# Activation copies put off, two early query blocks, and 1/rms taken with tokens on partitions, in a one-core decoder layer

## The chip, the cores and the metric

One core of one Trainium2 chip runs the whole program. The metric is the device time of one execution in microseconds (us); of several runs the median counts. The engines are named as in the profile: PE (TensorE, its weight loads shown apart as PEld), DVE (VectorE), ACT (ScalarE), POOL (GpSimd) and SP, whose queue issues most DMA transfers.

## The reference, cut to what matters

512 tokens, model width 1024, one layer:

```
h    = rmsnorm(x, norm1_g) * (1 + scale1) + shift1
p    = h @ w_in                          # q, k, v and the three conv inputs
attn = sliding-window attention(q, k, v) # 512 wide
conv = cb * short_conv(cc * cu)          # 512 wide
x    = x + gate1 * ([rmsnorm(attn) | rmsnorm(conv)] @ w_out)
h2   = rmsnorm(x, norm2_g) * (1 + scale2) + shift2
q    = h2 @ peer_wq                      # 8 heads x 2 halves x 128
sc   = q . subkeys                       # 128 scores per half, then top 16, pairs, top 16 again
x    = x + gate2 * sum over the chosen experts of softmax * gelu(u . h2) * v
```

with `rmsnorm(x, g) = x / sqrt(mean(x * x) + eps) * g`, the mean over the width of one token. Four such norms matter here: the first (over x), the conv norm, the attention norm (each 512 wide), and the second (over the updated x).

## The kernel before, in words

Activations lie transposed: the 128 partitions hold a block of the width, and the 512 tokens run along the free axis, so that `xT` is 8 tiles of 128x512. Products with a weight matrix are made exact enough by three passes: each factor is split into a rounded part and a rest (`split`, lines 175 to 177: ACT writes the rounded part, DVE the rest), and `mm3` (lines 197 to 202) issues three matmuls of 512 columns for each block of the depth. A block of 128 output columns therefore takes 24 matmuls. Weights come by SP's queue into five buffers and are split into four pairs of buffers.

A norm needs the sum of squares over the width, that is over partitions and blocks. Before, ACT squares the blocks, and a matmul with a 128x128 matrix of ones (lines 237, 253, 551 and 552) sums them over the partitions and at once repeats the sum on every partition, a 128x512 result in PSUM. `rstd` (lines 239 to 243) takes the square root of it on ACT and the reciprocal on DVE, both over 128x512, though all partitions hold the same 512 numbers.

The stages around the change, in order of the text:

- The first norm (from line 249), then the modulated activations `hH`, `hL`. The ones matmul stands on PE ahead of the matmuls that make the first modulation rows (`psr`, line 272).
- The input projection, attention and convolution follow the written list `PLAN` (line 50). `S` squares the conv output, `N` makes its norm (`part_norm`, line 463), `B2` and `B3` are the last two attention blocks (transposes, line 416, and products, line 425).
- The attention norm, squares and ones matmuls, at lines 518 to 520. Then `out_half(b, 0)`, the conv half of the output product, for four column blocks (48 matmuls), and `part_norm` of the attention half. The other half and the other blocks follow, each with its update of `xT` (line 544) and a running sum of squares.
- The second norm (lines 549 to 552 and 575). `spill` (line 528) transposes the updated x back, 32 transposes, and stores it. They wait for the last ones matmul (`end`).
- Then for each of 8 depth blocks `modulated` (line 226) makes `f` on DVE (x times scale times 1/rms), `fH` on ACT and `fL` on DVE. With `EARLY = 1`, one query block's three matmuls for that depth block follow at once on PE (line 582). Then `f` is transposed for two token groups (`pg`, line 593, 16 transposes), copied out, and 16 copies on ACT (line 598) put the first 352 tokens of `fH` and `fL` into `h2H` and `h2L`, which only `first()` (line 609, the u-side product of the experts) reads.
- The query loop (line 749), 16 turns: `query(hp)` makes the query block (24 matmuls), copies it out (`qs`, ACT), and `scores(hp - 1)` multiplies the block before with its subkeys (`psc`, line 739), copies the scores (ACT), and takes the top 16 of three token groups on DVE (`level1`, `level2`).
- After that the expert stages: `first`, `build`, `gated`, `second`, with gathered rows fetched by POOL.

The tile framework sets the waits and the order. A planner lays out each engine's instructions when the kernel is built, by its own model of durations. It goes by the order of the text where several instructions are ready, and takes a later one ahead where an earlier one still waits in its model. On the chip each engine then runs its list in that fixed order. PSUM has eight banks here: six of the pool `psm` (`bank`), two of `psa`.

Of the kernel before, what the change touches and what calls it, by code (L numbers as in the profile page):

```python
# [7 lines left out]
F32 = mybir.dt.float32  # L8
# [5 lines left out]
AF = mybir.ActivationFunctionType  # L14
# [4 lines left out]
P = 128  # L19
# [16 lines left out]
RING = 3  # L36
LOOK = 3
SPILL = 68
EARLY = 1
STB = 2  # L40
LD = 5
AHEAD = 7
# [47 lines left out]
def body(tc, p):  # L90
# [19 lines left out]
    def bank(name):  # L110
        return psm.tile([P, 512], F32, tag="m", name=name)
# [104 lines left out]
    def tmp(name):  # L216
        return tp.tile([P, T], F32, name=name, **T2)

    def squared(b, so_far=None):
        q = tmp("sq")  # L220
        nc.scalar.activation(q, b, AF.Square)
        if so_far is not None:
            nc.vector.tensor_add(q, q, so_far)
        return q
# [9 lines left out]
    def square(ps, b, i, n, w=None):  # L234
        q = tmp("sq")
        nc.scalar.activation(q, b, AF.Square)
        nc.tensor.matmul(ps, ones if w is None else w, q, start=(i == 0), stop=(i == n - 1))

    def rstd(ps, n):
        r = tmp("rstd")  # L240
        nc.scalar.activation(r, ps, AF.Sqrt, scale=1.0 / n, bias=eps)
        nc.vector.reciprocal(r, r)
        return r
# [2 lines left out]
    adabv = S("ada_b").rearrange("p (a k) -> p a k", a=6)  # L246


    ps = bank("ss1")
    sq = None  # L250
    for k in range(DC):
        sq = squared(xT[:, k, :], sq)
    nc.tensor.matmul(ps, ones, sq, start=True, stop=True)
    r1 = rstd(ps, D)
    hH = a1.tile([P, DC, T], F32R, tag="hH", name="hH")
    hL = a1.tile([P, DC, T], F32R, tag="hL", name="hL")
    hh, hlo = (lambda k: hH[:, k, :]), (lambda k: hL[:, k, :])
# [202 lines left out]
    vT = tmp("vT")  # L460
    nc.scalar.activation(vT, pj[5], AF.Copy)
    kg = S("kg")
    def part_norm(ss, src, g, o):
        r = rstd(ss, 512)
        for k in range(4):
            f = tmp("f")
            nc.vector.scalar_tensor_tensor(f, src[:, k, :], S(g, k), r, op0=OP.mult, op1=OP.mult)
            split(mH[:, o + k, :], mL[:, o + k, :], f)
# [12 lines left out]
    for step in PLAN.split():  # L481
        n = [int(x) for x in step[1:]]
        match step[0]:
            case "k":
                nk = qk1(pj[4], qk0(pj[4]), kg)
            case "q":
                nq[n[0]] = q0(pj[n[0]], n[0])
            case "P":
                pj[n[0]] = proj(n[0])
            case "V":  # L490
                pt = bank("vt")
                for c in range(NCH):
                    nc.tensor.transpose(pt[:, c * P:(c + 1) * P], vT[:, c * P:(c + 1) * P], ident)
                nc.scalar.activation(vN.rearrange("p a b -> p (a b)"), pt, AF.Copy)
            case "r":
                qk2(nq.pop(n[0]), qT[:, n[0], :])
            case "R":
                qk2(nk, kT)
            case "T":
                nc.scalar.activation(rq, ssq, AF.Sqrt, bias=eps64)  # L500
                nc.vector.reciprocal(rq, rq)
            case "A":
                sa[n[0]] = attend1(n[0])
            case "B":
                attend2(n[0], sa[n[0]])
            case "C":
                conv(*n)
            case "M":
                more_ada()
            case "S":  # L510
                ssc = bank("ssc")
                for k in range(4):
                    square(ssc, convT[:, k, :], k, 4)
            case "N":
                mH = a1.tile([P, DC, T], F32R, tag="hH", name="mH")
                mL = a1.tile([P, DC, T], F32R, tag="hL", name="mL")
                part_norm(ssc, convT, "cg", 0)
    ssa = bank("ssa")
    for k in range(4):
        square(ssa, attnT[:, k, :], k, 4)  # L520
    for b in range(HEAD):
        out_half(b, 0)
    part_norm(ssa, attnT, "ag", 4)
# [11 lines left out]
            nc.scalar.activation(xn, ps, AF.Copy)  # L535
            nc.sync.dma_start(x1s[c][:, half * 512:(half + 1) * 512], xn)

    ss2 = bank("ss2")
    sq = None
    for b in range(DC):  # L540
        if b >= HEAD:
# [6 lines left out]
        if b < 6:  # L548
            more_ada(3)
    sq = squared(xT[:, 6, :], sq)  # L550
    nc.tensor.matmul(ss2, ones, sq, start=True, stop=False)
    end = nc.tensor.matmul(ss2, ones, squared(xT[:, 7, :]), start=False, stop=True)
    nc.vector.tensor_add(mod[:, 24:48], mod[:, 24:48], ab[:, 24:48])
    nc.vector.scalar_tensor_tensor(s2, mod[:, 32:40], 1.0, S("n2g"), op0=OP.add, op1=OP.mult)
    a1_s.close()
# [16 lines left out]
    hx, hx_s = pool("hx")  # L572
    fH = hx.tile([P, DC, T], F32R, name="fH")
    fL = hx.tile([P, DC, T], F32R, name="fL")
    r2 = rstd(ss2, D)
    spill(0, end)
    spill(1, end)
    early = [(weights_of(p["wq"][b]), bank("pq")) for b in range(EARLY)]
# [5 lines left out]
    for r, (dst, cs) in enumerate(((hN, slice(TD - P, TD)), (h2N, slice(TD, T)))):  # L584
# [8 lines left out]
            nc.tensor.transpose(pg[k // 4][:, (k % 4) * P:(k % 4 + 1) * P], f[:, cs], ident)  # L593
        for k in range(2):
            nc.scalar.activation(dst[:, k * 512:(k + 1) * 512], pg[k], AF.Copy)
    for k in range(DC):
        for d, x in ((h2H, fH), (h2L, fL)):
            nc.scalar.activation(d[:, k, :], x[:, k, 0:TU].bitcast(F32), AF.Copy)

    xp_s.close()  # L600
    tp_s.close()
    r4, r4_s = pool("r4", side="right")
# [119 lines left out]
    def query(hp):  # L722
        sk = rp.tile([P, P], F32, tag="sk", name="sk", bufs=3)
        if hp < EARLY:
            ps = early[hp][1]
        else:
            w = weights_of(p["wq"][hp])
            ps = bank("pq")
            mm3(ps, w, lambda k: fH[:, k, :], lambda k: fL[:, k, :])
        nc.sync.dma_start(sk, p["sk"][hp])  # L730
        qs = tmp("qs")
        nc.scalar.activation(qs, ps, AF.Copy)
        return qs, sk
# [13 lines left out]

    last = None
    for hp in range(16):
        now = query(hp)  # L750
        if last:
            scores(hp - 1, *last)
        last = now
    scores(15, *last)
    weights(ND, Rd)
# [365 lines left out]
```

## Time and profile before

| | before |
|---|---|
| median of 3 runs | 1454.32 us (1452.81 to 1461.66) |
| profiled execution | 1453.08 us, of which span 1451.3 us |
| busy PE, PEld, DVE, ACT, POOL | 1394.5, 1224.8, 1240.8, 616.3, 405.3 us |
| from the start to the second norm's last ones matmul | 233.7 us |
| first subkey matmul of the query loop | at 258.8 us |

The span is the time between the first and the last recorded instruction of one profiled execution; 1.8 us of that execution lie around it. Busy time of PE is modelled at the ends of matmuls, which are pipelined: a busy PE can still have small stalls inside. A duration is that of one instruction, while the distance between the starts of two in a row is shorter where they overlap. A wait that the profile names is idle time of an engine, put down to what came last.

### The profile page before, as it was taken

The page shows a single profiled execution, that of the slowest core. Times are in us where ns is not written, and L with a number is a line of the kernel's source. Part 1 is how long each engine was busy: PE and PEld are TensorE (multiplying, and loading weights), DVE is VectorE, ACT ScalarE, POOL GpSimd, SP SyncE. Part 2 cuts the span into 40 slices and gives each one's busy share as a digit, 9 for nine tenths or more (in the row PEclk, how much of TensorE's full clock was granted, in tenths as well). Part 3 has the DMA queues.
Part 4 walks back from the last instruction along what each step waited for, and adds up shares of the span by engine and source line. Part 5 has one row for each costly group of instructions (what it writes and reads, how often), then busy time and mean ns, then how long its engine had stood idle before and what let it go on. Part 6 is the DMA issues. An engine that isn't in the chain of part 4 may idle for free.

```text
span 1451.3 us, 21225 instructions
## 1 busy us (share of the span) xinstructions
PE 1394.5 (96%) x7696; PEld 1224.8 (84%) x7696; DVE 1240.8 (85%) x2267; ACT 616.3 (42%) x1041; POOL 405.3 (28%) x292
## 2 busy tenths in 40 slices
PE   6999998999898999798999999999999999999998
PEld 4676776788898999798988888889899999999997
DVE  7778977899999999898568888988889898889944
ACT  4524636433634556364433333433343334333431
POOL 0000000000022320511024454446646455555300
PEclk9999999999999999999999999999999999999999
DMA  7645544222586997899989999999999999999843
GB/s 276 225 158 181 194 140 170 85 96 77 176 306 239 372 381 260 309 345 343 326 301 381 401 402 373 405 344 371 341 400 360 387 352 381 386 337 402 295 130 131
DMA packets 134376, 418.80 MB, mean 289 GB/s; under 512 B 12800, under 2 KB 39552, under 8 KB 132736
## 3 DMA queue, kind: packets, MB, share of 16 engines
q1 hardware_dynamic: 92800, 266.45, 51.1%
q0 software_dynamic: 41472, 151.01, 27.5%
q8 instruction: 60, 0.98, 0.3%
q14 instruction: 44, 0.36, 0.1%
HBM read 375.77 MB, written 41.62 MB: 288 GB/s over the span
## 4 chain that ended last, share of the span: by engine, by line
PE 22%; issue 14%; POOL 8%; DMA 7%; DVE 5%; ACT 0%; POOLq 0%; DVEq 0%; ACTq 0%
POOL row L773 8%; DMA row<-in_uR,eG 5%; PE pa L200 4%; PE pa L202 4%; PE pa L201 4%; PE o L990 3%; PE o L991 3%; PE o L989 3%; DMA row<-in_vL,eG 2%; DVE lo L177 2%; DVE junk L781 1%; DVE wwl L177 0%; DVE ga L905 0%; DMA raw<-in_vL 0%; DVE x L1008 0%
## 5 line engine op out<-in xcount | busy, mean ns | idle before, releaser
L176 ACT ACTIVATE hi<-raw 128x1024 fp32r<-128x1024 f32 x298 | 312.2, 1053 | 303.2 <-PE pa L201 83.9
L177 DVE TENSOR_TENSOR lo<-raw,hi 128x1024 fp32r<-128x1024 f32 x298 | 362.4, 1217 | 49.2 <-ACT hi L176 48.7
L200 PE MATMUL pa<-h2H,hi 128*128 128x352 f32 x1024 | 336.1, 328 | 21.1 <-ACT sp L621 21.1
L202 PE MATMUL pa<-h2H,lo 128*128 128x352 f32 x1024 | 332.8, 325 | 0.4 <-DVE lo L177 0.4
L201 PE MATMUL pa<-h2L,hi 128*128 128x352 f32 x1024 | 332.0, 324 | 0.0
L989 PE MATMUL o<-hi,wwh 128*128 128x512 f32 x768 | 299.5, 390 | 0.0
L990 PE MATMUL o<-lo,wwh 128*128 128x512 f32 x768 | 299.1, 389 | 0.2 <-DVE lo L177 0.2
L991 PE MATMUL o<-hi,wwl 128*128 128x512 f32 x768 | 298.9, 389 | 0.3 <-DVE wwl L177 0.3
L773 POOL DMA_INDIRECT row<-in_uR,eG x128 | 188.9, 1476 | 326.1 <-PE o L991 165.7
L781 DVE SCALAR_TENSOR_TENSOR junk<-row,h2N 128x1024 bf16<-128x1024 f32 x128 | 153.9, 1220 | 72.9 <-DMA row<-in_uR,eG 72.7
L200 PEld LDWEIGHTS pa<-h2H,hi 128*128 128x128 f32 x1024 | 194.8, 190 | 25.1 <-ACT sp L621 22.8
L773 POOL DMA_INDIRECT row<-in_vL,eG x128 | 171.7, 1341 | 145.6 <-PE o L991 91.3
L201 PEld LDWEIGHTS pa<-h2L,hi 128*128 128x128 f32 x1024 | 195.3, 191 | 2.2
L202 PEld LDWEIGHTS pa<-h2H,lo 128*128 128x128 f32 x1024 | 195.2, 191 | 0.7 <-DVE lo L177 0.7
L905 DVE SCALAR_TENSOR_TENSOR ga<-row,av,ga 128x1024 f32<-128x1024 f32 x127 | 163.0, 1283 | 25.6 <-DMA row<-in_vL,eG 24.5
L773 POOL DMA_INDIRECT row<-in_uR,eH x32 | 44.5, 1392 | 489.3 <-ACT sp L621 394.8
L991 PEld LDWEIGHTS o<-hi,wwl 128*128 128x128 f32 x768 | 144.1, 188 | 30.9 <-DVE wwl L177 0.7
L990 PEld LDWEIGHTS o<-lo,wwh 128*128 128x128 f32 x768 | 144.2, 188 | 28.7 <-DVE lo L177 0.6
L989 PEld LDWEIGHTS o<-hi,wwh 128*128 128x128 f32 x768 | 144.2, 188 | 28.2 <-issue 0.2
L176 ACT ACTIVATE wwh<-w 128x768 fp32r<-128x768 f32 x64 | 54.1, 845 | 156.9 <-DVE w L972 123.3
L971 ACT ACTIVATE w<-G 128x32 f32<-128x32 f32 x128 | 22.3, 222 | 196.3 <-DVE wwl L177 191.6
L177 DVE TENSOR_TENSOR wwl<-w,wwh 128x768 fp32r<-128x768 f32 x64 | 60.8, 951 | 10.5 <-ACT wwh L176 10.5
(265 smaller groups left out, 1831.2 us busy)
## 6 DMA issues: line engine op xcount, KB each, us to landing
raw<-in_uL SPq DMA_DIRECT2D x128, 512.0 KB, 6.2
raw<-in_vL SPq DMA_DIRECT2D x128, 512.0 KB, 6.9
Gd<-st SPq DMA_DIRECT2D x12, 2048.0 KB, 10.4
G<-Gd SPq DMA_DIRECT2D x16, 1536.0 KB, 11.7
ada<-in_ada SPq DMA_DIRECT2D x32, 512.0 KB, 4.2
Ad<-sp SPq DMA_DIRECT2D x34, 352.0 KB, 6.5
sp<-Ad SPq DMA_DIRECT2D x34, 352.0 KB, 7.1
raw<-in_w_in SPq DMA_DIRECT2D x18, 512.0 KB, 4.9
```

Source lines behind the costliest of these rows:

```text
L176: nc.scalar.activation(h, f, AF.Copy)
L177: nc.vector.tensor_sub(l, f, h.bitcast(F32))
L200: nc.tensor.matmul(ps, wh(k), rh(k), start=(k == k0), stop=False)
L201: nc.tensor.matmul(ps, wh(k), rl(k), start=False, stop=False)
L202: mark[0] = nc.tensor.matmul(ps, wl(k), rh(k), start=False, stop=(k == k1))
L773: d = nc.gpsimd.indirect_dma_start(out=t, out_offset=None, in_=tab, in_offset=bass.IndirectOffsetOnAxis(ap=e, axis=0))
L781: return nc.vector.scalar_tensor_tensor(junk, t, 1.0, h, op0=OP.mult, op1=OP.mult, accum_out=a)
L905: nc.vector.scalar_tensor_tensor(ga, t, av[:, k:k + 1], ga, op0=OP.mult, op1=OP.add)
L971: nc.scalar.activation(wv[:, i, nu:], g[:, i, nu:], AF.Copy)
L989: nc.tensor.matmul(o, wh[:, cs], vh[:, hs], start=(j == 0), stop=False)
L990: nc.tensor.matmul(o, wh[:, cs], vl[:, hs], start=False, stop=False)
L991: last = nc.tensor.matmul(o, wl[:, cs], vh[:, hs], start=False, stop=(j == NJ - 1))
```

## The change

Three edits. `EARLY` goes from 1 to 2, so that two query blocks accumulate while the second norm's activations are made. The 16 copies into `h2H` and `h2L` leave their place behind the transposes and go into the query loop, two behind the scores of each turn from the third to the tenth, each with a wait for the last product matmul that stood in the text ahead of that turn's query block. And the four norms over the width (first, conv, attention, second) use `token_rstd`: the squares are the stationary factor and one column of ones the moving one, chunk of 128 tokens by chunk, so that the sums come out with tokens on partitions, 128x4. The square root and the reciprocal work on 128x4. A product with the identity spreads these numbers on diagonals (`dg`, 128x512), and one matmul with ones repeats them on all partitions in a PSUM bank, which the users then read. The attention norm's squares stay where they were, but its matmuls now stand in `part_norm`, behind the 48 matmuls of the four half products; those of the conv norm stand in `N`, behind `B2`. The q and k norms are as before.

```diff
--- before.py
+++ after.py
@@ -36,7 +36,7 @@
 RING = 3
 LOOK = 3
 SPILL = 68
-EARLY = 1
+EARLY = 2
 STB = 2
 LD = 5
 AHEAD = 7
@@ -236,6 +236,27 @@
         nc.scalar.activation(q, b, AF.Square)
         nc.tensor.matmul(ps, ones if w is None else w, q, start=(i == 0), stop=(i == n - 1))
 
+    def token_rstd(qs, n, pl):
+
+
+        ps = bank("ss")
+        for c in range(NCH):
+            for i, q in enumerate(qs):
+                end = nc.tensor.matmul(ps[:, c:c + 1], q[:, c * P:(c + 1) * P], ones[:, 0:1], start=(i == 0),
+                                       stop=(i == len(qs) - 1))
+        r = cp.tile([P, 16], F32, tag="r", name="r", bufs=2)[:, 0:NCH]
+        nc.scalar.activation(r, ps[:, 0:NCH], AF.Sqrt, scale=1.0 / n, bias=eps)
+        nc.vector.reciprocal(r, r)
+        dg = tmp("dg").rearrange("p (c n) -> p c n", c=NCH)
+        sd = [P, NCH, P]
+        nc.vector.tensor_mul(dg, ident[:, None, :].to_broadcast(sd), r[:, :, None].to_broadcast(sd))
+        out = pl()
+        nc.tensor.matmul(out, ones, dg, start=True, stop=True)
+        return out, end
+
+    def psa_bank():
+        return psa.tile([P, 512], F32, tag="a", name="rr")
+
     def rstd(ps, n):
         r = tmp("rstd")
         nc.scalar.activation(r, ps, AF.Sqrt, scale=1.0 / n, bias=eps)
@@ -246,12 +267,10 @@
     adabv = S("ada_b").rearrange("p (a k) -> p a k", a=6)
 
 
-    ps = bank("ss1")
     sq = None
     for k in range(DC):
         sq = squared(xT[:, k, :], sq)
-    nc.tensor.matmul(ps, ones, sq, start=True, stop=True)
-    r1 = rstd(ps, D)
+    r1, _ = token_rstd([sq], D, lambda: bank("rr"))
     hH = a1.tile([P, DC, T], F32R, tag="hH", name="hH")
     hL = a1.tile([P, DC, T], F32R, tag="hL", name="hL")
     hh, hlo = (lambda k: hH[:, k, :]), (lambda k: hL[:, k, :])
@@ -460,8 +479,15 @@
     vT = tmp("vT")
     nc.scalar.activation(vT, pj[5], AF.Copy)
     kg = S("kg")
-    def part_norm(ss, src, g, o):
-        r = rstd(ss, 512)
+    def squares(src):
+        qs = []
+        for k in range(4):
+            qs.append(tmp("sq"))
+            nc.scalar.activation(qs[k], src[:, k, :], AF.Square)
+        return qs
+
+    def part_norm(qs, src, g, o):
+        r, _ = token_rstd(qs, 512, psa_bank)
         for k in range(4):
             f = tmp("f")
             nc.vector.scalar_tensor_tensor(f, src[:, k, :], S(g, k), r, op0=OP.mult, op1=OP.mult)
@@ -508,16 +534,12 @@
             case "M":
                 more_ada()
             case "S":
-                ssc = bank("ssc")
-                for k in range(4):
-                    square(ssc, convT[:, k, :], k, 4)
+                ssc = squares(convT)
             case "N":
                 mH = a1.tile([P, DC, T], F32R, tag="hH", name="mH")
                 mL = a1.tile([P, DC, T], F32R, tag="hL", name="mL")
                 part_norm(ssc, convT, "cg", 0)
-    ssa = bank("ssa")
-    for k in range(4):
-        square(ssa, attnT[:, k, :], k, 4)
+    ssa = squares(attnT)
     for b in range(HEAD):
         out_half(b, 0)
     part_norm(ssa, attnT, "ag", 4)
@@ -535,7 +557,6 @@
             nc.scalar.activation(xn, ps, AF.Copy)
             nc.sync.dma_start(x1s[c][:, half * 512:(half + 1) * 512], xn)
 
-    ss2 = bank("ss2")
     sq = None
     for b in range(DC):
         if b >= HEAD:
@@ -548,8 +569,7 @@
         if b < 6:
             more_ada(3)
     sq = squared(xT[:, 6, :], sq)
-    nc.tensor.matmul(ss2, ones, sq, start=True, stop=False)
-    end = nc.tensor.matmul(ss2, ones, squared(xT[:, 7, :]), start=False, stop=True)
+    r2, end = token_rstd([sq, squared(xT[:, 7, :])], D, psa_bank)
     nc.vector.tensor_add(mod[:, 24:48], mod[:, 24:48], ab[:, 24:48])
     nc.vector.scalar_tensor_tensor(s2, mod[:, 32:40], 1.0, S("n2g"), op0=OP.add, op1=OP.mult)
     a1_s.close()
@@ -572,7 +592,6 @@
     hx, hx_s = pool("hx")
     fH = hx.tile([P, DC, T], F32R, name="fH")
     fL = hx.tile([P, DC, T], F32R, name="fL")
-    r2 = rstd(ss2, D)
     spill(0, end)
     spill(1, end)
     early = [(weights_of(p["wq"][b]), bank("pq")) for b in range(EARLY)]
@@ -593,10 +612,6 @@
             nc.tensor.transpose(pg[k // 4][:, (k % 4) * P:(k % 4 + 1) * P], f[:, cs], ident)
         for k in range(2):
             nc.scalar.activation(dst[:, k * 512:(k + 1) * 512], pg[k], AF.Copy)
-    for k in range(DC):
-        for d, x in ((h2H, fH), (h2L, fL)):
-            nc.scalar.activation(d[:, k, :], x[:, k, 0:TU].bitcast(F32), AF.Copy)
-
     xp_s.close()
     tp_s.close()
     r4, r4_s = pool("r4", side="right")
@@ -747,9 +762,13 @@
 
     last = None
     for hp in range(16):
+        so_far = mark[0]
         now = query(hp)
         if last:
             scores(hp - 1, *last)
+            if 2 <= hp < 2 + DC:
+                for d, x in ((h2H, fH), (h2L, fL)):
+                    after(nc.scalar.activation(d[:, hp - 2, :], x[:, hp - 2, 0:TU].bitcast(F32), AF.Copy), so_far)
         last = now
     scores(15, *last)
     weights(ND, Rd)
```

## Rows read from the trace of the kernel before

**Rows 1.** Page, part 1: busy us (share of the span) and instructions.
```profile
PE 1394.5 (96%) x7696; PEld 1224.8 (84%) x7696; DVE 1240.8 (85%) x2267; ACT 616.3 (42%) x1041; POOL 405.3 (28%) x292
```
**Rows 2.** Waits of PE, whole span: us in total, times, longest us.
```profile
PE pa L200 <- ACT sp L621: 21.1, 7, 6.6
```
**Rows 3.** Windows of 50 us: length, busy of each engine, PE clock, DMA, GB/s.
```profile
300.00:350.00 50.00, 50.00 (x253) 42.21 (x251) 49.52 (x278) 16.19 (x31) 0.00 (x0) 1.00 0.27 83
750.00:800.00 50.00, 50.00 (x222) 41.41 (x221) 39.31 (x52) 17.94 (x28) 20.50 (x17) 1.00 1.01 385
```
**Rows 4.** Timeline, second norm: start us, us, instruction, [idle before <- releaser].
```profile
231.94 0.63 ACT L221 ACTIVATE sq<-xT 128x512 f32<-128x512 f32 x1
232.62 1.12 PE L552 MATMUL ss<-sq,ones 128*128 128x512 f32 x2 [0.65 <-ACT sq L221]
233.58 3.66 PE L532 MATMUL xt<-cst,xT 128*128 128x128 f32 x32
234.51 3.35 DVE L242 RECIPROCAL rstd<-rstd 128x512 f32<-128x512 f32 x1 [1.22 <-ACT rstd L241]
237.90 2.08 DVE L229 SCALAR_TENSOR_TENSOR f<-xT,s,rstd 128x512 f32<-128x512 f32 x3
239.62 0.50 PE L200 MATMUL pq<-fH,hi 128*128 128x512 f32 x1 [2.38 <-ACT fH L230]
```
**Rows 5.** Groups by line, 238 to 259 us: busy us, mean ns | idle.
```profile
L231 DVE SCALAR_TENSOR_TENSOR fL<-f,mod,fH 128x512 fp32r<-128x512 f32 x8 | 5.9, 748 | 0.1
L598 ACT ACTIVATE h2H<-fH 128x352 fp32r<-128x352 f32 x8 | 3.9, 490 | 0.0
L593 PE MATMUL pg<-cst,f 128*128 128x128 f32 x16 | 2.8, 276 | 0.0
```
**Rows 6.** Timeline: weight loads, the second query block's end, first subkey matmuls.
```profile
220.79 12.86 SPq L181 DMA_DIRECT2D raw<-in_wq  x5
...
255.88 0.39 PE L202 MATMUL pq<-fH,lo 128*128 128x512 f32 x1
...
258.78 1.16 PE L739 MATMUL psc<-sk,qs 128*128 128x128 f32 x8 [2.51 <-ACT qs L732]
...
265.28 1.05 PE L739 MATMUL psc<-sk,qs 128*128 128x128 f32 x8
```
**Rows 7.** Waits of ACT, 262 to 350 us: us in total, times, longest us.
```profile
ACT hi L176 <- PE pq L201: 59.6, 14, 4.3
```
**Rows 8.** Windows of 2 us, columns as in rows 3 (clock third from last).
```profile
180.00:182.00 2.00, 0.00 (x0) 0.00 (x0) 2.00 (x4) 2.00 (x4) 0.00 (x0) 1.00 0.59 227
182.00:184.00 2.00, 1.82 (x3) 0.79 (x4) 2.00 (x3) 1.49 (x4) 0.00 (x0) 0.57 0.00 0
242.00:244.00 2.00, 2.00 (x6) 1.66 (x6) 2.00 (x4) 2.00 (x6) 0.00 (x0) 0.57 0.68 259
```
**Rows 9.** Timeline, attention norm, from the last attention products to the first update.
```profile
178.62 1.31 PE L425 MATMUL po<-pT,vN 128*64 128x128 f32 x16
182.18 5.40 PE L237 MATMUL ssa<-sq,ones 128*128 128x512 f32 x8 [2.24 <-ACT sq L236]
188.33 3.35 DVE L242 RECIPROCAL rstd<-rstd 128x512 f32<-128x512 f32 x1 [2.32 <-ACT rstd L241]
192.69 2.07 DVE L467 SCALAR_TENSOR_TENSOR f<-attnT,sm,rstd 128x512 f32<-128x512 f32 x3
201.24 0.75 DVE L544 SCALAR_TENSOR_TENSOR xT<-py,mod,xT 128x512 f32<-128x512 f32 x1 [2.62 <-PE py L202]
```
**Rows 10.** Nearest rows to what is new: timeline, 54 to 90 us.
```profile
56.66 2.12 PE L357 MATMUL ssq<-cs,sq 128*128 128x2 f32 x16 [0.83 <-ACT sq L355]
...
86.39 0.29 ACT L500 ACTIVATE rq<-ssq,eps 128x32 f32<-128x32 f32 x1 [1.80 <-PE ssq L357]
```
**Rows 11.** Groups by line, 164 to 181 us: the conv norm's ones matmuls.
```profile
L237 PE MATMUL ssc<-sq,ones 128*128 128x512 f32 x8 | 3.9, 605 | 0.5 <-ACT sq L236 0.5
```
**Rows 12.** Timeline, first norm: what DVE does after its reciprocal.
```profile
20.75 0.29 DVE L290 SCALAR_TENSOR_TENSOR pick<-psr,cst 128x128 f32<-128x128 f32 x1 [0.66 <-PE psr L272]
```

## The prediction

> **What bounds the kernel.** I read the busy times first: PE works in 96% of the span, DVE in 85% [rows 1]. Then the windows, since a share over all stages says little: in the query loop PE and DVE are both full (50.00 and 49.52 of 50 us), and in the expert stage PE is full and DVE is not [rows 3]. What PE still waits for after the loop is mostly the gelu output, 21.1 us in 7 waits [rows 2]. Those waits hang on transfers and instructions that were issued shortly before them, so they move with the work. The rule I draw: after the query loop has begun, PE and DVE carry a fixed load to the end, and a us by which that loop starts earlier is a us off the time. So the change is worth what it does to the start of the loop, the first subkey matmul at 258.78 [rows 6], and the four norms count as far as they move PE ahead of it.
>
> All sums are against the profiled execution, 1453.08 us (span 1451.3 and 1.8 around it). It lies 1.2 us under the median of the runs, 1454.32.
>
> **Second norm, early blocks, copies.** Before: the last square is done at 232.57; two ones matmuls, square root and a reciprocal of 3.35 us bring the first `f` at 237.90, 5.33 us later [rows 4]. After, in place of that:
> - 16 matmuls of one column: the nearest row has 16 of two columns in 2.12 us, 0.1325 each [rows 10], so 2.1.
> - The square root on 128x4: 0.3, as on 128x32 [rows 10]. The reciprocal on 128x4 has no row here; it lies between nothing and 3.35, and I take 0.3 as for the root, since its size is that of the small row.
> - `dg`, 128x512 on DVE: 0.75, as `fL` [rows 5].
> - The repeating matmul, two passes of 512 columns: 1.1, as the pair in [rows 4].
> - Five handovers at some 0.05, an estimate from 232.57 to 232.62 [rows 4]: 0.25.
>
> Sum 4.8, so `f` comes at about 237.4, half a us earlier. The users read 1/rms from PSUM instead of SBUF; I take the same duration, as the update `xT` reads PSUM at 0.75 [rows 9] and `fL` reads SBUF at 0.748 [rows 5].
>
> PE: the small sums end near 234.7, the 32 transposes take 3.66 [rows 4], the repeating matmul 1.1, so it is free at 239.5. Before, it waited 2.38 for `fH` until 239.62 [rows 4]; that wait goes, and PE's own work is late next. Then come 8 steps. One block's three matmuls take 0.68: between two subkey groups lie 24 matmuls and 8 small ones of 1.05 together, (265.28 - 258.78 - 1.05)/24 = 0.227 each [rows 6]. Before, DVE set the pace with two instructions of 0.75 a step [rows 5], and PE stood idle half the time. With two blocks a step asks 1.36 of PE and up to 1.5 of DVE: the second block's 5.45 us lie beside DVE's work. PE then has 48 x 0.227 = 10.9 and the 16 `pg` transposes at 0.114 [rows 4, 5], 1.8: 239.5 + 12.7 = 252.2. DVE is done by 237.4 + 8 x 1.5 = 249.4.
>
> The weights of the second block cost nothing: five query loads are issued from 220.79 on [rows 6], so load and split are over by then, and no DMA is pushed ahead of another. If that cover were gone, a load and a split would stand ahead of step one.
>
> The 16 copies stood on ACT between the activations and `qs`, and PE, done at 256.3, waited 2.51 for `qs` [rows 6]. They leave that path. In the loop ACT waits 59.6 us in 14 turns for PE, up to 4.3 a turn [rows 7]; two copies take 2 x 0.49 = 1.0 [rows 5]. Their added wait is for a product matmul that ends before the `qs` that ACT has already copied, so what is queued behind them (the next split) does not wait longer. They cost nothing beside that idle time; without that cover, 7.8.
>
> So the first subkey matmul comes at some 252.3 instead of 258.78: **-6.5**. Ends: -8.3, if the `pg` transposes fall behind it; -2.0, if `qs` again waits 2.5 on ACT [rows 6] and PE's clock costs the 2.0 told of below.
>
> **Conv norm.** 8 ones matmuls of 3.9 us [rows 11] become 32 small ones, 32 x 0.1325 = 4.2, and the repeating pair, 1.1. They stand between the last attention blocks, where PE is the one that works through: **+1.4**. Ends 0 (they fall into stalls that the modelled busy time hides) and +1.4. DVE's reciprocal of 3.35 becomes some 1.1; its result is not wanted before PE is through B3.
>
> **Attention norm.** Before: PE ends the attention products at 179.93, waits 2.24 for squares, takes 5.40 for their sums, and starts the half products at 187.6 [rows 9]: 7.65 lost, but the reciprocal then hides beside 48 half products (10.9). After: the half products start when the conv half is split, say 0.8 after B3. Then 4.2 of small sums, and in the open root 0.3, reciprocal 0.3, `dg` 0.75, repeating matmul 1.1, handovers 0.25, `f` 0.75 and its rounding 0.65: 4.1. That is -7.65 + 0.8 + 4.2 + 4.1 = **+1.4**. I take this order because the text puts the sums behind the 48, and those are ready. Ends: -2.3, if the planner takes the sums ahead of the 48 (4.2 + 1.1 against 7.65, the rest hidden); +5.9, by the last rival.
>
> **First norm.** 8 small sums add 1.1 to PE, DVE loses 2.3 of work. But its next instruction, `pick`, waited for PE, not for the reciprocal [rows 12]. Ends -2.3 and +1.1; I take **0**, between them.
>
> **Sum**: -6.5 + 1.4 + 1.4 + 0 = -3.7, so 1449.4.
>
> **The rivals.**
> 1. *The norms pass their relief on.* The planner puts the attention sums ahead of the half products and the first norm frees DVE: -6.5 + 0 - 2.3 - 1.2 = -10.0, so 1443; all best ends give 1440. For it: DVE loses some 9 us over four norms, and PE's 7.65 hole is wide open. Against: the order of the text.
> 2. *The clock stays low in the early blocks.* PE ran at 0.57, the 1.2 GHz level, at 242 to 244 [rows 8], after transposes and an idle 2.38 [rows 4], and at 182 to 184 after an idle 2.24 [rows 8, 9]. In the early blocks that was free, because DVE paced them; now PE paces them. I forecast that without the idle time the clock stays at 2.4 GHz. If transposes alone let it fall, some 4 us run at half rate: +2.0, so 1451.4. The Trainium skill, "TensorE: Matmul & The Clock Gate", Part 4, says that transposes do not count as activity for the clock as matmuls do; by that rule this rival holds. These rows have transposes and idle time together and can't part the two.
> 3. *Nothing is gained.* DVE bounds the loop and the stages after it, and a new plan gives the time back in the gelu waits; one such wait is up to 6.6 [rows 2]. Then 1453. Against: DVE's top-16 work starts earlier by as much as PE's.
> 4. *Slower: the attention norm in the open.* The chain after the small sums leaves PE idle for 3.0 (4.1 less the repeating matmul), longer than the 2.24 after which the clock fell [rows 8, 9]: the next 4 us at half rate, +2.0. And if PE takes the second halves block by block, it waits for the last of four attention parts. DVE needs 8 x 0.75 = 6.0 for `f` and rest of the four parts [rows 5], and PE's block would end some 0.5 after that, at 6.5, where the sum has 1.4 for the first part and 2.7 for the block's matmuls: +2.4, say 2.5. So this norm costs 1.4 + 4.5 = 5.9, and the whole -6.5 + 1.4 + 5.9 = +0.8: 1453.9. It decides once the loop starts less than 7.3 earlier; with the -4.5 of rival 2 it gives 1456.
>
> **The numbers.** Forecast 0.45 (its own range 1446 to 1452), rival 1 0.22, rival 2 0.13, rival 3 0.08, rival 4 0.12. Range 1440 to 1457, from the best ends of rival 1 to rival 4 with a us of spread. About 1% (14.5 us) is what a measurement tells from no change here. No case reaches +14.5; 0.03 for one that I don't see. Below 1439.8 lies only the tail of rival 1, with a plan that also shortens the gelu waits: 0.11. The rest, 0.86, is within 1%.
>
> **What would show it.** First subkey matmul near 252; no wait for `fH` ahead of the early blocks; `h2H` copies spread over the loop beside ACT's waits; the granted clock at 239 to 244; 32 small sums behind the 48 half products with a hole of some 3 us on PE. Wrong, if the loop starts earlier by much more or less than 6.5 less the delays, or if its lead is not found again at the end.

## The result and the profile after

The changed kernel takes 1468.19 us (median of 7 runs, 1463.26 to 1471.06), the one before 1454.32: a ratio of 1.0093 (95% interval 1.0077 to 1.0109), 13.5 us slower. My forecast was 1449.4 in a range of 1440 to 1457. It was wrong. The loop edits did most of what was forecast of them; the four norms cost some 17 us, where I had priced them at 2.3 (1.4 + 1.4 + 0, and -0.5 for the second).

The profiled execution took 1468.2 us, span 1466.3. Busy times, as in [rows 1]; PE has 12 us more, DVE 8 less:

```profile
PE 1406.8 (96%) x7770; PEld 1239.5 (85%) x7770; DVE 1232.5 (84%) x2271; ACT 615.1 (42%) x1041; POOL 411.0 (28%) x292
```

How much later each milestone comes after than before, in us: first `pick` (it takes the modulation rows out of `psr`) +2.8, first projection product +2.8, the root for q's norm +6.9, last conv output +8.9, last attention products +12.8, last update of `xT` +14.9, first `f` of the second norm +15.4, first subkey product **+9.8**. From 357 to 690 us the offset stays within +8.5 and +11.5, and by 1360 to 1401 us it is +15. So the norms lose 15.4 ahead of the loop, the loop edits win 5.6 back, and 5 more go late.

**First norm** (timeline: start us, us, instruction, [idle before <- releaser]), to hold against [rows 12]:

```profile
13.65 1.81 PE L245 MATMUL ss<-ones,sq 128*128 128x1 f32 x8 [3.98 <-DVE sq L223]
15.32 4.61 PE L291 MATMUL psr<-raw,ccol 128*128 128x256 f32 x10
16.00 0.69 DVE L252 TENSOR_TENSOR dg<-cst,r 128x512 f32<-128x512 f32 x1
19.73 1.45 PE L254 MATMUL rr<-dg,ones 128*128 128x512 f32 x2
21.01 1.46 PE L291 MATMUL psr<-raw,ccol 128*128 128x256 f32 x6
21.21 1.29 DVE L314 TENSOR_TENSOR f<-xT,rr 128x512 f32<-128x512 f32 x2 [4.52 <-PE rr L254]
22.42 1.22 DVE L177 TENSOR_TENSOR lo<-raw,hi 128x1024 fp32r<-128x1024 f32 x1
23.55 0.28 DVE L309 SCALAR_TENSOR_TENSOR pick<-psr,cst 128x128 f32<-128x128 f32 x1
...
60.45 1.86 PE L376 MATMUL ssq<-cs,sq 128*128 128x2 f32 x11 [3.54 <-ACT sq L374]
```

The diagonal is ready at 16.7, but the repeating product `rr` stands behind ten modulation products and ahead of the last six, which `pick` needs. DVE, kept waiting 4.52, does two `f` and a split (`lo`) first, and comes to `pick` at 23.55, before at 20.75. Later PE waits 3.54 for q's squares, where it waited 0.83 [rows 10].

**Conv norm and attention norm**, against [rows 9, 11]:

```profile
180.71 0.83 PE L245 MATMUL ss<-ones,sq 128*128 128x1 f32 x6
182.05 1.95 PE L245 MATMUL ss<-ones,sq 128*128 128x1 f32 x16
187.56 1.16 PE L254 MATMUL rr<-dg,ones 128*128 128x512 f32 x2
...
203.00 3.63 PE L245 MATMUL ss<-ones,sq 128*128 128x1 f32 x32
206.67 0.26 ACT L248 ACTIVATE r<-ss,eps 128x4 f32<-128x4 f32 x1 [10.54 <-PE ss L245]
206.96 0.18 DVE L249 RECIPROCAL r<-r 128x4 f32<-128x4 f32 x1 [5.09 <-ACT r L248]
207.18 0.69 DVE L252 TENSOR_TENSOR dg<-cst,r 128x512 f32<-128x512 f32 x1
207.92 1.73 PE L254 MATMUL rr<-dg,ones 128*128 128x512 f32 x2 [1.29 <-DVE dg L252]
211.16 2.07 PE L200 MATMUL py<-mH,hi 128*128 128x512 f32 x4 [1.50 <-ACT mH L176]
218.08 0.75 DVE L565 SCALAR_TENSOR_TENSOR xT<-py,mod,xT 128x512 f32<-128x512 f32 x1 [2.47 <-PE py L202]
```

From the first small sum to the first product of the attention half are 8.16 us, in which PE runs nothing else.

**Second norm and loop start**, against [rows 4, 6]:

```profile
247.50 1.72 PE L245 MATMUL ss<-ones,sq 128*128 128x1 f32 x14 [1.46 <-ACT sq L221]
249.08 2.86 PE L554 MATMUL xt<-cst,xT 128*128 128x128 f32 x13
251.73 1.50 PE L254 MATMUL rr<-dg,ones 128*128 128x512 f32 x2
253.27 2.07 DVE L229 SCALAR_TENSOR_TENSOR f<-xT,s,rr 128x512 f32<-128x512 f32 x3 [2.81 <-PE rr L254]
266.85 1.91 PE L612 MATMUL pg<-cst,f 128*128 128x128 f32 x16
268.60 1.06 PE L754 MATMUL psc<-sk,qs 128*128 128x128 f32 x8
```

No wait for `qs` is left ahead of the subkey products, and `f` to subkey product is 15.3 us, before 20.9.

**Windows of 2 us** (columns as in rows 3, granted clock third from last), against [rows 8]:

```profile
16.00:18.00 2.00, 2.00 (x6) 1.57 (x5) 0.69 (x1) 0.94 (x1) 0.00 (x0) 0.50 0.68 254
186.00:188.00 2.00, 2.00 (x9) 1.34 (x10) 0.00 (x0) 0.14 (x1) 0.00 (x0) 0.54 0.39 158
212.00:214.00 2.00, 2.00 (x6) 1.52 (x6) 2.00 (x4) 0.42 (x1) 0.00 (x0) 0.50 0.00 0
250.00:252.00 2.00, 2.00 (x11) 2.00 (x10) 0.46 (x1) 1.43 (x3) 0.00 (x0) 0.50 0.67 262
256.00:258.00 2.00, 2.00 (x9) 1.66 (x10) 2.00 (x4) 2.00 (x6) 0.00 (x0) 1.00 0.40 155
```

In this execution PE is at or near 0.50 of its clock, the 1.2 GHz level, behind each norm's sums, while the early blocks (256 to 258) have the full 2.4. Summed over the first 300 us, the time at the low level (a window of 2 us at clock c counts 4 x (1 - c)) is 34.1 us, before 13.6.

### The profile page after: what moved, and what is told of

It is laid out like the page before. It is cut to its first block, busy times and chain, and to the rows that moved or that the text cites. A ratio compares the mean times of both kernels' runs of the same rounds, so it can differ in the third digit from the quotient of the medians.

```text
span 1466.3 us, 21381 instructions
## 1 busy us (share of the span) xinstructions
PE 1406.8 (96%) x7770; PEld 1239.5 (85%) x7770; DVE 1232.5 (84%) x2271; ACT 615.1 (42%) x1041; POOL 411.0 (28%) x292
## 4 chain that ended last, share of the span: by engine, by line
PE 35%; issue 8%; DMA 6%; DVE 5%; POOL 4%; ACT 0%; POOLq 0%; SPq 0%; DVEq 0%; ACTq 0%
PE o L1010 7%; PE o L1009 7%; PE o L1008 7%; PE pa L200 5%; PE pa L202 5%; PE pa L201 4%; POOL row L792 4%; DMA row<-in_uR,eG 3%; DMA row<-in_vL,eG 3%; DVE lo L177 1%; DVE junk L800 1%; DVE B L958 1%; DMA Gd<-st 1%; DVE wwl L177 0%; DVE x L1027 0%
## 5 line engine op out<-in xcount | busy, mean ns | idle before, releaser
L792 POOL DMA_INDIRECT row<-in_vL,eG x128 | 178.9, 1398 | 143.1 <-PE o L1010 80.4
```

Source lines behind the costliest of these rows:

```text
L792: d = nc.gpsimd.indirect_dma_start(out=t, out_offset=None, in_=tab, in_offset=bass.IndirectOffsetOnAxis(ap=e, axis=0))
```

## The experiments

Each ratio is to the kernel before, run beside it on the same chip (its medians there: 1453.3 to 1454.5). "By the ratio" means (ratio - 1) x 1454.3. An interval reaches 2 to 4 us to either side (4.7 in one run), so one difference of two kernels is known to some 3 to 5 us.

Two theories. **Clock**: one-column products let the clock fall, and the work behind them runs at half rate. **Chain**: the new way puts sums, root, diagonal and repeating product in a row behind the last square, and that row lies in the open.

### The parts of the change

*Loop edits alone* (kernel before):

```diff
-EARLY = 1
+EARLY = 2
...
-            nc.scalar.activation(d[:, k, :], x[:, k, 0:TU].bitcast(F32), AF.Copy)
...
+                    after(nc.scalar.activation(d[:, hp - 2, :], x[:, hp - 2, 0:TU].bitcast(F32), AF.Copy), so_far)
```

> The kernel before with two early query blocks and the copies in the loop; all norms as before. Theory (the norms cost what was lost, the loop edits do what was forecast): the first subkey matmul about 6 us earlier than in the kernel before, the rest moves with it, 1447 to 1450 us. Rival (the loop edits themselves upset the later stages, where the changed kernel lost its last 5 us): the lead is gone or turned round by the end, 1454 to 1460.

1450.04 us, 0.9973 (0.9956 to 0.9989): 3.9 us under the kernel before, clear of the interval, though small. It beats both kernels.

*Norms alone* (changed kernel, `EARLY = 1`, the copies in their old place):

> The kernel before with the four norms taken with tokens on partitions; one early block, copies at their old place. Theory: the second norm's squares come 15 us later, as in the changed kernel, and nothing is won back: 1469 to 1476 us. Rival (the loop edits carry part of the loss): 1455 to 1465.

1472.93, 1.0134 (1.0102 to 1.0167). So the norms carry the whole loss.

*Copies alone*, and *second early block alone* (each one of the two edits above, on the kernel before):

> The kernel before with the sixteen copies in the query loop and nothing else. By my forecast's working the copies held back the first copied query block by 2.5 us, and the second early block is worth the other 4: the first subkey product 2.5 us earlier from the first normed block on, 1451 to 1452. If the two only work together (the second block's products fill the time that the copies took on the scalar engine), it is 0 to 1: 1453 to 1454.

> The kernel before with two early query blocks, the sixteen copies in their old place. The loop edits together gave 4.0 us between the first normed block and the first subkey product, the copies alone 2.7. If the two add up, the second block alone gives 1.3 there: 1452 to 1453. If the copies hold the first copied query block by as much as the second block is early, it gives nothing: 1453 to 1454. My forecast's working gave it 4.

Copies alone: 1450.21, 0.9980 (0.9965 to 0.9996); the subkey product comes 2.7 us sooner after the first `f`. The block alone: 1455.95, 1.0010 (0.9993 to 1.0026), no gain, and short of both expectations. First subkey product, copies alone and then block alone:

```profile
256.30 1.05 PE L735 MATMUL psc<-sk,qs 128*128 128x128 f32 x8
```

```profile
258.00 2.07 PE L739 MATMUL psc<-sk,qs 128*128 128x128 f32 x8 [5.94 <-ACT qs L732]
```

PE's wait for `qs` is 2.51 before [rows 6]. The copies take it away; the second block without them makes it 5.94, because PE is done sooner and ACT is not.

### One norm at a time

Each puts one norm of the changed kernel back, by the lines that the diff removed for it: first, conv, attention, second.

> The changed kernel with its first norm alone put back to the 128-column product and the root and reciprocal on 512 columns. In the changed kernel the first projection product stands 2.8 us later than before, the first weights of the attention 6.9 us later. Clock theory (streams of one-column products are followed by half-rate stretches): the half-rate stretch at 12 to 20 us goes, these two markers come back to within 1 us of before, and the time falls by 3 to 7 us, to 1461 to 1465. Chain theory (only the added products and their waits cost): the first projection product comes back by 2.8 us, the later markers by no more than that, 1465 to 1466.

1461.77, 1.0069 (1.0046 to 1.0092): 3.5 less than the changed kernel by the ratios, 6.4 by the medians, at the edge of what can be told. The wait for q's squares is short again:

```profile
55.59 2.12 PE L378 MATMUL ssq<-cs,sq 128*128 128x2 f32 x16 [0.83 <-ACT sq L376]
```

> The changed kernel with the convolution's norm alone put back. In the changed kernel the products between the first weights of the attention and the last attention output lose 6.6 us. Clock theory: the half-rate stretch at 184 to 188 us goes and 4 to 7 us come back, 1461 to 1464. Chain theory: only the added products and the wait for the diagonal come back, 1 to 2 us, 1466 to 1467.

1467.63, 1.0093 (1.0067 to 1.0119): no gain in time. The clock theory's 4 to 7 are missed; the chain theory's 1 to 2 can't be told from none. The trace does show a gain: from the last conv output to the last attention products are 11.06 us, as in the kernel before, where the changed kernel takes 14.95. This profiled execution (1473.09) loses it again in other stages.

> The changed kernel with the attention's norm alone put back to four 128-column products before the half products. The changed one lost 3.3 us between the last attention output and the first new residual row. Clock theory: the half-rate stretch at 208 to 215 us goes and 3 to 4 us come back, 1464 to 1465. Chain theory: the norm's chain is out of the open (8.2 us of small sums, root, diagonal, repeating product, division against the 4 products of before): also about 3 us. The two differ by the clock of the stretch behind it alone. A gain under 1 us would speak against both.

1460.81, 1.0050 (1.0029 to 1.0072): 6.3 by the ratios, twice what either theory had, though 3 to 4 lies within the error of the difference.

> The changed kernel with the second norm alone put back to two 128-column products and the root and reciprocal on 512 columns. In the changed kernel the way from the last new residual row to the first normed block is 0.5 us longer than before, where I forecast 0.5 us shorter. Both theories: within 1.5 us of the changed kernel, 1467 to 1470; the chain theory leans to a gain of 0.5, the clock theory to none, since the stretch behind this norm is short of products with or without it.

1469.12, 1.0108 (1.0082 to 1.0134): no difference that can be told.

The other way round, norms added to the loop edits: the second; then conv too.

> The loop edits with the new second norm alone; the other three norms as before. My forecast's term: 0.5 us less than with the old second norm, so 1449.5. Clock theory: PE is short of products there with either norm, so no half-rate stretch is added: 1449 to 1451. Chain theory: the repeating product behind the transposes puts the first normed block no earlier: 1450 to 1451.

> The changed kernel with the first and the attention norm put back, so both loop edits with the new conv norm and second norm. If the four norms' costs are independent (first 6.4, attention 7.4, conv 0.6, second -0.9 by the runs that put each back): 1468.2 - 13.8 = 1454.4, though the kernel with the loop edits alone stood at 1450.0. If they are not (each norm's low clock counts once for whatever stands behind it), it goes to that kernel's time: 1449 to 1451. A version to beat both.

1452.80, 0.9987 (0.9973 to 1.0001), and 1456.37, 1.0025 (1.0011 to 1.0040): short of the forecast's 0.5 us gain, and nearer to costs that add than to costs that overlap. The changed kernel without its new first norm is the next step, so there is a ladder by the ratios: loop edits -3.9; second norm +2.0; conv +5.5; attention +6.4; first +3.5; sum +13.5. Each step is known to some 3 to 4 us. The conv norm's place in it is uncertain, since putting it back gave nothing in time.

### Clock or chain

*Small sums 128 columns wide* (same sums, same order):

```diff
-                end = nc.tensor.matmul(ps[:, c:c + 1], q[:, c * P:(c + 1) * P], ones[:, 0:1], start=(i == 0),
+                end = nc.tensor.matmul(ps[:, c * P:(c + 1) * P], q[:, c * P:(c + 1) * P], ones, start=(i == 0),
...
-        nc.scalar.activation(r, ps[:, 0:NCH], AF.Sqrt, scale=1.0 / n, bias=eps)
+        nc.scalar.activation(r, ps[:, 0:T:P], AF.Sqrt, scale=1.0 / n, bias=eps)
```

> The changed kernel with small sums of 128 columns instead of one: same weight loads, 128 columns streamed for each. Clock theory (one-column matmuls let PE's clock fall to 1.2 GHz at each norm): the granted clock stays up after the sums of at least the conv and the attention norm, 1456 to 1463 us. Chain theory (the loss is the chain of root, diagonal and repeating matmul in the open, and the added matmuls): the same time as the changed kernel within 2, 1466 to 1470, or some 2 more, for the columns.

1462.15, 1.0061 (1.0040 to 1.0082). Time at the low level falls to 17.1 us. The attention norm's sums take as long as in the changed kernel, but the clock stays up behind them; timeline, then windows:

```profile
199.17 3.73 PE L245 MATMUL ss<-ones,sq 128*128 128x128 f32 x32
```

```profile
206.00:208.00 2.00, 1.18 (x4) 0.67 (x4) 2.00 (x5) 1.80 (x3) 0.00 (x0) 1.00 0.00 0
208.00:210.00 2.00, 1.95 (x9) 1.61 (x9) 1.89 (x4) 0.17 (x2) 0.00 (x0) 1.00 0.00 0
```

From the last conv output to the last attention products are 11.06 us in all six profiles with the old conv norm, 14.95 to 17.60 in the seven with the new one as in the changed kernel, and 11.92 and 11.95 with wide sums. So what the new conv norm costs there, 3.9 and more, is for the most part the clock.

*The attention norm's chain ahead of the 48 half products*, alone and then with wide sums:

```diff
-    ssa = squares(attnT)
+    ssa, _ = token_rstd(squares(attnT), 512, psa_bank)
```

> The changed kernel with the attention norm's small sums, root and repeating matmul ahead of the 48 half products instead of behind them. Chain theory: the chain hides beside the half products, the last update of x comes 4 to 6 us earlier than in the changed kernel, 1462 to 1464. Clock theory: the half-rate stretch only moves in front of the half products, and the gain is 1 to 3: 1465 to 1467.

> The changed kernel with both edits tried one by one before: the small sums 128 columns wide, and the attention norm's sums, root and repeating product ahead of the 48 half products. Apart they gave 6.0 and 4.5 us. If the clock and the open chain are two losses, they add up: 1457 to 1459, and no stretch at half rate lies in the half products as it did with the chain ahead alone. If the chain ahead only helped by where the low clock fell, the two overlap: 1461 to 1463. What is left over before by then is the first norm's (6.4 us by the run that put it back): the first weights of the attention still 4 us late.

1463.71, 1.0065 (1.0042 to 1.0088), and 1461.05, 1.0056 (1.0039 to 1.0073). Ahead gives 4.1 by the ratios with one-column sums, 0.7 with wide ones: the two seem to overlap, though the error of each is as large as the 3.4 between them, and with wide sums moving this chain is worth little.

*Sums without the chain, the chain without sums, wide sums without the chain, neither*. In the first, behind the sums:

```diff
+        out = tmp("dg")
+        nc.vector.tensor_copy(out, ones[:, 0:1].to_broadcast([P, T]))
+        nc.vector.scalar_tensor_tensor(out[:, 0:NCH], ps[:, 0:NCH], 0.0, ones[:, 0:NCH], op0=OP.mult, op1=OP.add)
```

The second reads `qs[-1][:, 0:NCH]` in the root and has no sums; the fourth reads the same in the DVE instruction above.

> The changed kernel with the one-column sums of all four norms, and behind them no root, reciprocal, diagonal or repeating product: the users multiply by ones (the norms are left out of the result), after one DVE instruction that reads the sums. Clock theory: the half-rate stretches behind the sums stay, 1459 to 1464. Chain theory: only the products that the sums replaced are left, with no reciprocal behind them, 1446 to 1453.

> The changed kernel without the sums: the root reads four columns of the last square (the sums are left out of the result), and reciprocal, diagonal and repeating product follow as in the changed kernel, in the same places. Clock theory: no one-column products, so no half-rate stretch beyond those of before, and PE is spared 10 us of sums: 1444 to 1452. Chain theory: the waits for the diagonal and the first norm's late repeating product stay, 1455 to 1462.

> The kernel with sums and no chain (the norms are left out of the result, as there), its sums 128 columns wide instead of one. With the chain behind them wide sums gave 6.0 us. If the low clock costs that by itself, they give 5 to 6 here too: 1450 to 1451. If the low clock only costs what stands behind it in a chain, they give 0 to 2: 1454 to 1456.

> The changed kernel with neither sums nor chain: the users multiply by ones behind one DVE instruction that reads the last square (the norms are left out of the result). If sums and chain were two costs that add, it would stand 5 under the chain alone and 4 under the sums alone less their overlap: 1438 to 1442. If each alone is nearly hidden and only the two in a row lie in the open, it stands close under both: 1446 to 1452.

1455.93, 1454.03, 1450.43 and 1443.01. The first two lie between the theories; wide sums give what the clock theory asked for; the kernel with neither lies 1 us above the range of costs that add, and 3 under the other. In these four the stretch from the first subkey product to the end is 1192.6 to 1198.9 us, with the norms 1192.5 before and 1197.7 after: their times differ for the most part by what comes ahead of the loop, and not by the values that the missing norms change later. All six together, us against before by the ratio (interval of the ratio):

| | no chain | chain |
|---|---|---|
| no sums | -9.7 (0.9911 to 0.9955) | -1.9 (0.9967 to 1.0008) |
| wide sums | -2.8 (0.9965 to 0.9998) | +8.9 (1.0040 to 1.0082) |
| one-column sums | +1.2 (0.9991 to 1.0024) | +13.5 (1.0077 to 1.0109) |

Read down: wide sums cost 7 to 11, and one column instead of 128 costs 4.0 more without the chain and 4.6 with it, each known to some 3.5. Read across: the chain costs 8 to 12. Neither theory alone holds. Alone, one-column sums cost 10.9 and the chain 7.8, together 18.7; in the changed kernel both cost 23.2. The 4.5 between lie within the error, so the costs add or come to somewhat more. The old norms, in the kernel with the loop edits alone (-3.9), cost 5.8 against none at all, so the new ones lose 23.2 - 5.8 = 17.4. Windows behind the attention norm's sums, one-column and then wide, both without the chain:

```profile
202.00:204.00 2.00, 2.00 (x7) 1.52 (x6) 2.00 (x4) 0.49 (x1) 0.00 (x0) 0.50 0.00 0
```

```profile
200.00:202.00 2.00, 2.00 (x10) 1.58 (x9) 1.30 (x3) 0.63 (x1) 0.00 (x0) 1.00 0.00 0
```

That the clock goes with the columns holds for these two norms. In all profiles together, the clock behind one-column sums is at 0.50 in eight of eight at the conv norm and in seven of seven at the attention norm, and at 1.00 behind wide sums in three of three at each. At the other two norms it comes and goes with any kind: behind the first norm's sums it is at 0.50 in four of seven profiles with one column, one of three with wide sums and three of seven with the old ones; at the second norm in seven of nine with one column and one of three with wide sums, and a few us behind the old ones in five of five. (Wide sums also shift the planner's order a little: in the first norm `rr` stands behind 12 products in place of 10.)

PE's busy time at sums is not what grew: 88 small ones take 11.5 us in the changed kernel, the 20 old ones took 13.5 (2.1, 3.9, 5.4 and 2.1 by their lines); the repeating products add 5.8. What the table prices beside the clock is their place. The likely reason, argued and not tested by itself: each old product summed one square as it came, while a small sum needs all squares of its norm for its first column, so that all of them stand behind the last square. That can hold for the conv and the attention norm; the first has a single square tile before and after.

## Why the prediction was wrong

**Second norm, blocks, copies: -6.5 forecast, -5.1 measured** in the changed kernel, from the last update of `xT` to the first subkey product. Of it, -6.0 was forecast behind `f` and -5.6 came; the rest is the next point. The time of the loop edits alone has -3.9. Mechanism right: no wait for `qs`, two blocks in the time of DVE's steps. Its division was wrong: I gave 2.5 to the copies and 4 to the block, and the block alone gives nothing; beside the copies it gives 1.4 in the traces, too little to be told in the times.

**Second norm's `f`: 0.5 earlier forecast.** From the last sums' start to `f` are 5.77 us after and 5.28 before. The sums were even shorter than I had them (0.11 each, not 0.13). I had summed the chain as if PE were free for its last link; on PE's list 13 transposes stand ahead of `rr`, here at half rate. With the attention norm put back, the same list ran at full clock, and `f` came 4.90 us after the last update, against 5.99 before and 6.49 in the changed kernel; so the half rate, and not the place, made it late:

```profile
240.72 1.61 PE L556 MATMUL xt<-cst,xT 128*128 128x128 f32 x13
```

```profile
242.00:244.00 2.00, 2.00 (x15) 1.42 (x13) 0.78 (x3) 0.96 (x2) 0.00 (x0) 1.00 0.75 291
```

**Attention norm: +1.4 forecast, about +6.4 by the ladder.** The chain was right in place and size: 8.16 measured, 4.2 + 4.1 forecast. What failed is what I put behind it, a block of products in 2.7. From the first product to the first update are 6.92 us, at the low clock (0.50) and with waits for the parts of the attention half (1.50 at its start). That is rival 4, told there with its price of 5.9, and I gave it 0.12. With wide sums and the clock at 1.00 the chain takes 7.65 and this stretch 5.46:

```profile
206.82 1.21 PE L200 MATMUL py<-mH,hi 128*128 128x512 f32 x4 [1.50 <-ACT mH L176]
...
212.28 0.75 DVE L565 SCALAR_TENSOR_TENSOR xT<-py,mod,xT 128x512 f32<-128x512 f32 x1 [1.00 <-PE py L202]
```

So the low clock costs 2.0 here, as the rival had it, and the waits for the parts 5.46 - 2.7 = 2.8, where it had 2.4. Its condition, an idle PE, was not what decided: with wide sums PE idles as long for the diagonal (1.29) and the clock stays at 1.00, and in the kernel with the loop edits alone the wait of 2.24 for the squares is there too, with the clock at 1.00 behind it. The trace shows less of this norm than the ladder: from the last attention products to the first update 4.0 us more than before, and by the last update 2.0 of these are won back. Where the rest of the 6.4 arises stays open.

**Conv norm: +1.4 forecast, as PE time.** By the ladder +5.5, in the trace +3.9 between the last conv output and the last attention products. I added instructions and left out what they do to those behind: the last block's transposes and products run at 0.54 to 0.60. With wide sums only 0.9 of the 3.9 is left.

**First norm: 0 forecast, +3.5 by the ladder.** I had seen rightly that the old reciprocal was hidden beside `psr`, and so had nothing to give. But I counted only the small sums on PE, and not that `rr` goes into PE's list ahead of products that `pick` waits for, nor that DVE, while it waits, is handed work ahead of `pick`. That makes the 2.8. The low clock has no part in it: with the attention norm's chain ahead the clock was at 1.00 here, and `pick` came 9.79 us after DVE's last sum of squares, with 0.50 in the changed kernel 9.96, before 6.90.

The step from 2.8 to 6.9 is another thing. PE's wait for q's squares is 3.3 to 3.6 us in all 12 kernels with a new first norm of any kind, also in the one with neither sums nor chain, whose `pick` is 3.1 earlier than before; with the old first norm it is 0.6 to 0.8 in all seven. ACT loads a table for a sine ahead of these squares. In the changed kernel it does so 0.5 us before PE is through with the products ahead of them (at 56.91), behind a split that had waited for PE; in the kernel with neither also 0.5 before (50.42); in the kernel before 4.6 before (55.82). The wait in the kernel with neither, then the table loads of all three, in this order:

```profile
54.00 3.58 PE L367 MATMUL ssq<-cs,sq 128*128 128x2 f32 x16 [3.58 <-ACT sq L365]
```

```profile
56.41 1.28 ACT L343 ACT_TABLE_LOAD   x1
```

```profile
49.95 1.28 ACT L334 ACT_TABLE_LOAD   x1
```

```profile
51.19 1.28 ACT L324 ACT_TABLE_LOAD   x1
```

So it goes with another order of ACT's work, which the plan takes once the old first norm is gone, and not with sums, chain or clock. Why the plan changes there stays open.

**The failing step** is thus the pricing of the norms. I priced them by instructions added to PE, at full clock, at 2.3 together; the terms that came out wrong most are conv (+1.4), attention (+1.4) and first (0). The runs show 17.4 in their place: sums and chain cost 23.2 where the old norms cost 5.8, and 4 to 4.6 of that goes with the one-column sums and the low clock behind them. In three of the four norms the old reciprocal of 3.35 was hidden, and its removal is worth nothing, while what replaces it on PE isn't hidden. Only in the second norm it stood on the path ([rows 4]: it ends at 237.86, `f` starts at 237.90).

**The other rivals.** Rival 1 is false: where the attention chain does go ahead, there is no such gain. Rival 2 is false for the changed kernel, whose early blocks run at 1.00: its low stretch fell earlier, into transposes and `rr`. In the kernel with the loop edits and the old norms it holds, and from `f` to the subkey product that kernel gains 4.0, near the 4.5 told there:

```profile
238.00:240.00 2.00, 1.94 (x6) 1.50 (x6) 2.00 (x5) 2.00 (x5) 0.00 (x0) 0.52 0.47 180
```

The Trainium skill, "TensorE: Matmul & The Clock Gate", Part 4, says that transposes don't count as activity for the clock as matmuls do. The trace of the loop edits agrees as far as it can tell, since an idle time of 2.74 lies there too. By itself the rule doesn't decide: with the attention norm put back the same 32 transposes stand behind one-column sums, and the clock stays at 1.00 (window above). Nor is it what cost the changed kernel: wide sums change no transpose, and took half of the low time away.

**That a lead at the loop start is found again at the end** holds to 1170 us (+8.5 to +11.5). After that the changed kernel loses 5 more. In the waits of PE from 1000 to 1440 us, the changed kernel and then the one before (`pa` and `o` are products of the expert stages):

```profile
PE pa L202 <- DVE lo L177: 2.0, 2, 1.1
PE o L1009 <- DVE lo L177: 1.9, 2, 1.0
```

```profile
PE pa L202 <- DVE lo L177: 0.4, 1, 0.4
PE o L990 <- DVE lo L177: 0.2, 1, 0.2
```

No run puts that down to an edit: in the profiled execution of the new second norm on the loop edits, at 1457.28 well over its median of 1452.80, 8 us are lost between 700 and 1400 us. What sets it from run to run stays open. So the causes above rest on the times of several runs, and on the milestones of one profile only where these agree.

## What to carry to other kernels

Price a replaced step by the row of waits from the last input to the first user, and look which link of the old one was on the path: a long instruction that is hidden gives nothing back. Products that each take one input as it comes can hide their cost where the same sum taken at the end can't; that is argued here, not tested by itself. When two edits go together, try each alone: by the traces, one of these two worked only beside the other.

## What was not expected of the hardware

At the conv and the attention norm, streams of 32 fp32 products with one moving column were followed by PE's 1.2 GHz level in all 15 cases profiled, although the profile shows PE busy in them; the same products 128 columns wide took as long (32 in 3.73 us against 3.63) and were followed by 2.4 GHz in all six. With all four norms changed, wide sums are worth 4 to 4.6 us by the ratios. Behind the shorter streams of the first and the second norm either level was seen with either width. A reciprocal over 128x4 takes 0.18 us, one over 128x512 3.35.
